# Half-width products and masked copies in the recurrence levels of a hybrid decoder layer

## The chip, the cores and the metric

The kernel runs on one core of one Trainium2 chip. The metric is device time in microseconds (us) of one execution. Before the change three runs gave 2996.32, 3003.64 and 3007.43 us; the median is 3003.64 us. One further execution was profiled and took 3003.55 us, of which 3001.8 us lie between its first and its last instruction (the span).

## The reference, cut to what matters

One decoder layer over 1024 tokens of width 1024: normalise, project to q, f, i, g (four heads of 128 columns each) and u, run a gated linear recurrence (HGRN2) on the heads and a state-space scan (S5) on u, project out, normalise again, and add a mixture of retrieved expert rows (PEER). The change touches only the recurrence of the heads:

```python
f = lb + (1 - lb) * sigmoid(f_logit);  log_f = log(f);  k = 1 - f
bcum = cumsum(lc, axis=2)                    # within a chunk
decay = exp(where(causal, bcum_t - bcum_s, -inf))
scores = einsum('bhtk,bhsk,bhtsk->bhts', qc, kc, decay)
o_intra = einsum('bhts,bhsv->bhtv', scores, vc)
...
new_state = exp(b_last) * state + einsum('bhsk,bhsv->bhkv', kc * exp(b_last - bcum), vc)
o = rmsnorm(o_inter + o_intra) * silu(g)
```

## The kernel before, in words

Tokens are handled in four chunks of 256 columns (`CHUNKS`). `hgrn_in` makes the tiles f, k, b (the running sum of log f), q, gg and v of one piece, `hgrn_out` the recurrence of that piece. A piece is 512 columns wide, which is four blocks (`NB2` = 4) of 128 tokens: one head of chunks 0 and 1 together, or two heads of chunk 2 or 3. So there are eight calls of `hgrn_out`: four for chunks 0 and 1 and two each for chunks 2 and 3.

The scores of a block are a 128 x 128 table (source token s on the partitions, target token t along the columns). Since the decay can't be split into a factor of s and a factor of t without overflow, `hgrn_out` builds the table in eight levels, `a` = 0 to 7. At level a below 7 the tokens are cut into runs of `lsz` = 2^a; pairs of neighbouring runs are treated with the end of the earlier run as reference point. The tile xx holds, in the later run of each pair, q times the decay since the reference point (line 735), and in the earlier run, k times the decay up to it (line 736); at level 0 these are f times q (line 726) and a copy of k (line 727). TensorE multiplies xx with itself, block by block (line 741, tile hg in PSUM), and VectorE copies out of the 128 x 128 result those entries whose s lies in an earlier run and whose t lies in the later run of the same pair, by a mask of bytes, into the table sc (line 742). Level 7 is the diagonal: k times q under the mask of the identity. Two PSUM tiles of the name hg turn over, so the product of level a + 2 waits for the copy of level a. After the levels come the decays over a block (lines 745 to 751), a transpose (754), the state (759 to 767) and the output products (770, 771).

Each float32 product appears in the trace as two matrix instructions, each with its own weight load; 4 blocks x 7 levels x 8 calls = 224 products are 448 instructions, and the diagonal adds 64.

The pieces of chunks 0 and 1 are called between the S5 groups; after that `ORDER` gives the sequence: pieces of chunk 2 beside the output projection and second normalisation of chunk 0 (`o0 N0`), pieces of chunk 3 beside those of chunk 1. That is the order of the calls only: the program is built with `schedule_with_timeline_sim=True`, so a planner with estimated costs sets the order of the instructions on each engine when the kernel is built. Each engine then works its own list in order and waits on semaphores for the others.

Names in the rows below: `proj` (line 326) is every projection with 256 columns; `rstd_fin` (lines 231 to 249) is the chain of small VectorE steps for 1/sqrt; line 272 makes the diagonal matrices `diag` out of it, with which line 286 normalises and transposes; line 807 adds the output projection to x; line 971 is the product of a gathered expert row with h2; lines 1040, 1041 and 1076 belong to the dense part of the experts.

Of the kernel before, what the change touches and what calls it, by code (L numbers as in the profile page):

```python
# [22 lines left out]
P = 128  # L23
# [66 lines left out]
def hymba_kernel(  # L90
# [22 lines left out]
    nc = tc.nc  # L113
# [3 lines left out]
    def T(pool, shape, dt, tag, bufs=None):  # L117
        return pool.tile(shape, dt, name=f"{tag}_{next(cnt)}", tag=tag, bufs=bufs)
# [5 lines left out]
    def bc(ap, axis, n):  # L124
        a = ap.unsqueeze(axis)
        shape = list(a.shape)
        shape[axis] = n
        return a.to_broadcast(shape)
# [81 lines left out]
    def pair(pool, dt=F32, tag="tmp", bufs=4):  # L210
        return T(pool, [P, 2, TC], dt, tag, bufs=bufs)
# [15 lines left out]
    def rstd_fin(pool, ms, n, w):  # L227

        W = lambda dt: T(pool, [P, n], dt, "rstd", bufs=9)
        m = W(F32)  # L230
        TS(m, ms, 1.0 / w, EPS, ALU.mult, ALU.add)
        i = W(I32)
        TS(i, m.bitcast(I32), -0.5, 1597463007.0, ALU.mult, ALU.add)
        y = i.bitcast(F32)
        z = W(F32)
        TT(z, m, y, ALU.mult)
        for r in range(3):
            u = W(F32)
            if r < 2:

                STT(u, z, -0.5, y, ALU.mult, ALU.mult)
            else:
                STT(u, y, -0.5, y, ALU.mult, ALU.mult)
                TT(u, u, m, ALU.mult)
            y2 = W(F32)
            STT(y2, u, 1.5, y, ALU.add, ALU.mult)
            if r == 0:
                z2 = W(F32)
                STT(z2, u, 1.5, z, ALU.add, ALU.mult)
                z = z2  # L250
            y = y2
        return y
# [378 lines left out]
    sts, scs, hc = [], [], {}  # L631
# [34 lines left out]
    NB2 = 2 * NBC  # L666
    B4 = lambda t: t.rearrange("p (c t) -> p c t", t=P)
# [42 lines left out]
    def hgrn_out(hp, last, h, tiles, one, dst):  # L710
        f, k, b, q, gg, v = tiles
        W = lambda tag, bufs=None: T(hp, [P, W2], F32, tag, bufs=bufs or NH.get(tag, 2))
        PB = lambda tag: T(ps, [P, BANK], F32, tag, bufs=2)
        blk = lambda t, c: t[:, c * P : (c + 1) * P]
        sc = scs[0]
        for a in range(8):
            lsz = 1 << a
            pt = PB("hg")
            if a < 7:
                two = lambda t: t.rearrange("p (n two l) -> p n two l", two=2, l=lsz)  # L720
                bv, qv, kv = two(b), two(q), two(k)
                n = W2 // (2 * lsz)
                xx = W("xx")
                xv = two(xx)
                if a == 0:
                    TT(xv[:, :, 1, :], two(f)[:, :, 1, :], qv[:, :, 1, :], ALU.mult)
                    nc.vector.tensor_copy(xv[:, :, 0, :], kv[:, :, 0, :])
                else:
                    z = W("z")
                    zv = two(z)  # L730
                    ref = bv[:, :, 0, lsz - 1 : lsz].to_broadcast([P, n, lsz])
                    TT(zv[:, :, 1, :], bv[:, :, 1, :], ref, ALU.subtract)
                    TT(zv[:, :, 0, :], ref, bv[:, :, 0, :], ALU.subtract)
                    ACT(z, z, AF.Exp)
                    TT(xv[:, :, 1, :], zv[:, :, 1, :], qv[:, :, 1, :], ALU.mult)
                    TT(xv[:, :, 0, :], zv[:, :, 0, :], kv[:, :, 0, :], ALU.mult)
                lh, rh = xx, xx
            else:
                lh, rh = k, q
            for c in range(NB2):  # L740
                nc.tensor.matmul(blk(pt, c), blk(lh, c), blk(rh, c), start=True, stop=True)
            nc.vector.copy_predicated(sc, bc(hc["masks"][:, a, :], 1, NB2), B4(pt))

        e = W("e", 1)
        ACT(e, b, AF.Exp)
        qd = W("xx")
        TT(qd, q, e, ALU.mult)
        z = W("z")
        TT(B4(z), B4(b)[:, :, P - 1 : P].to_broadcast([P, NB2, P]), B4(b), ALU.subtract)
        ACT(z, z, AF.Exp)  # L750
        TT(z, z, k, ALU.mult)
        pk = PB("tr")
        for c in range(NB2):
            nc.tensor.transpose(blk(pk, c), blk(z, c), ident)
        kd = W("kd", 1)
        nc.scalar.copy(kd, pk)
        pst = PB("hg")
        for c in range(NB2):
            nc.tensor.matmul(blk(pst, c), blk(kd, c), blk(v, c), start=True, stop=True)

        sth = W("sth", 1)
        nb = NB2 if one else NBC
        before = []
        for c in range(NB2):
            src = sts[h + c // nb] if c % nb == 0 else blk(sth, c - 1)
            before.append(src)
            STT(blk(sth, c), src, e[:, c * P + P - 1 : c * P + P], blk(pst, c), ALU.mult, ALU.add)
        po = PB("hg")
        for c in range(NB2):
            nc.tensor.matmul(blk(po, c), blk(qd, c), before[c], start=True, stop=False)  # L770
            nc.tensor.matmul(blk(po, c), sc[:, c, :], blk(v, c), start=False, stop=True)
        if not last:
            for i in range(NB2 // nb):
                nc.vector.tensor_copy(sts[h + i], blk(sth, (i + 1) * nb - 1))
        osq = W("z")
        ACT(osq, po, AF.Square)
        ms = T(tp, [P, NB2], F32, "ms", bufs=3)
        nc.vector.tensor_reduce(ms, B4(osq), AX.X, ALU.add)
        r = rstd_fin(tp, ms, NB2, P)
        on = W("xx")  # L780
        TT(B4(on), B4(po), bc(r, 2, P), ALU.mult)
        pt = PB("tr")
        for c in range(NB2):
            nc.tensor.transpose(blk(pt, c), blk(on, c), ident)
        mx = dst if dst is not None else pair(tp, F32, "mixr", 4)
        STT(mx.rearrange("p h t -> p (h t)"), pt, gnw, gg, ALU.mult, ALU.mult)
        return mx
# [49 lines left out]
    for o, i, ni, j, nj in pieces_:  # L837
        n = max(ni, nj)
# [388 lines left out]
    def head_pieces(c, two=False):  # L1227

        t = {}
        outs = []  # L1230
        far = T(gp, [P, 2, 2, TC], F32, "acc") if c == 2 else None

        def last(h):
            outs.append(hgrn_out(hp, c == NCK - 1, h, t.pop(h), two, None if far is None else far[:, h // 2]))
            if not two:
                raws.setdefault(c, []).append((outs[-1][:, 0], outs[-1][:, 1]))

        for h in range(0, HEADS, 1 if two else 2):
            if len(t) == 2:
                last(min(t))  # L1240
                yield
            t[h] = hgrn_in(hp, h, hTs[c], hTs[c + 1] if two else None)
            yield
        for h in sorted(t):
            last(h)
            yield
        if two:
            for i in range(2):
                raws[c + i] = [(outs[h][:, i], outs[h + 1][:, i]) for h in range(0, HEADS, 2)]
# [188 lines left out]
```

## Time and profile before

| | before |
|---|---|
| median of three runs | 3003.64 us |
| profiled execution | 3003.55 us, span 3001.8 us |
| TensorE busy | 2793.9 us, 93% of the span |
| weight loads busy | 2500.6 us, 83% |
| VectorE busy | 2480.9 us, 83% |
| ScalarE busy | 1095.5 us, 36% |
| GpSimd busy | 1108.5 us, 37% |
| mean granted TensorE clock | 0.973 |

How to read it: busy time is the sum over the instructions of an engine, with overlaps counted once. Matrix instructions are pipelined: one takes some 0.275 us from start to end, while the next starts much earlier, so the distance between starts, not the duration, is the price of one. "PE" is TensorE's matrix row, "PEld" its row of weight loads, DVE is VectorE, ACT ScalarE, POOL GpSimd. [...]

### The profile page before, as it was taken

To read this page: it belongs to the slowest core of one execution; us is meant where nothing else is said; L and a number is where in the kernel's file an instruction comes from. 1 tells how busy PE (TensorE), PEld (TensorE's weight loads), DVE (VectorE), ACT (ScalarE), POOL (GpSimd) and SP (SyncE) were. 2 spreads that over 40 slices of the span, in tenths; PEclk is the share of its full clock that TensorE was granted. 3 is DMA by queue.
4 is the path that set the end of the run, shared out by engine and by line. 5 is a ranking of instruction groups with operands and counts; after the bars stand their busy time and mean duration, and the time that the engine had idled before them with its cause. 6 is when DMAs were issued, how large, how long until landed. Compare 5 with 4: busy or idle time off the path is not lost.

```text
span 3001.8 us, 46134 instructions
## 1 busy us (share of the span) xinstructions
PE 2793.9 (93%) x16071; PEld 2500.6 (83%) x16071; DVE 2480.9 (83%) x5606; ACT 1095.5 (36%) x2406; POOL 1108.5 (37%) x1043
## 2 busy tenths in 40 slices
PE   6898979988989799999999999999999999999995
PEld 5677878877878789999998888888888888888874
DVE  7869844987799999997667888888888888888998
ACT  4223431422310688996623322222222222222222
POOL 1764100231112002333344444445545454535553
PEclk9899999999999899999999999999999999999998
DMA  9722334685766358998999999889999898999986
GB/s 335 262 81 66 105 116 155 211 300 189 249 228 187 119 189 305 330 358 320 372 332 352 331 315 329 301 304 360 341 345 317 314 325 310 328 316 329 309 318 231
DMA packets 376265, 816.69 MB, mean 272 GB/s; under 512 B 60128, under 2 KB 153952, under 8 KB 370912
## 3 DMA queue, kind: packets, MB, share of 16 engines
q0 software_dynamic: 110592, 402.70, 38.2%
q1 hardware_dynamic: 227248, 388.74, 37.4%
q10 hardware_dynamic: 38192, 22.31, 2.6%
q8 instruction: 126, 2.06, 0.3%
q14 instruction: 107, 0.88, 0.1%
HBM read 732.27 MB, written 81.36 MB: 271 GB/s over the span
## 4 chain that ended last, share of the span: by engine, by line
PE 35%; DVE 20%; issue 18%; DMA 14%; POOL 10%; ACT 3%; ACTq 0%; POOLq 0%; DVEq 0%; SPq 0%
PE mm L1076 15%; POOL row L946 8%; PE mm L326 8%; DMA row<-in_v_rows_dram,ei 5%; PE s L1152 3%; DVE row L971 3%; PE tr L1152 2%; PE hg L1152 2%; DMA row<-in_u_rows_dram,ei 2%; DMA vraw<-in_v_rows_dram 2%; DVE acc L987 2%; ACT oL L1036 1%; DMA S<-sd 1%; PE s L1040 1%; PE s L1041 1%
## 5 line engine op out<-in xcount | busy, mean ns | idle before, releaser
L1076 PE MATMUL mm<-h2T,w 128*128 128x320 f32 x6144 | 958.7, 315 | 43.2 <-ACT S L1078 33.0
L1076 PEld LDWEIGHTS mm<-h2T,w 128*128 128x128 f32 x6144 | 925.9, 192 | 55.4 <-ACT S L1078 38.8
L946 POOL DMA_INDIRECT row<-in_u_rows_dram,ei x384 | 452.0, 1177 | 1166.8 <-DVE dots L971 711.5
L946 POOL DMA_INDIRECT row<-in_v_rows_dram,ei x384 | 494.8, 1288 | 525.1 <-DVE acc L987 422.5
L326 PE MATMUL mm<-hT,w 128*128 128x256 f32 x2304 | 531.5, 385 | 3.3 <-ACT tmp L610 2.7
L987 DVE SCALAR_TENSOR_TENSOR acc<-row,dots,acc 128x1024 f32<-128x1024 f32 x381 | 487.8, 1280 | 36.4 <-DMA row<-in_v_rows_dram,ei 33.3
L326 PEld LDWEIGHTS mm<-hT,w 128*128 128x128 f32 x2304 | 435.1, 194 | 61.0 <-ACT tmp L610 3.1
L971 DVE CUSTOM_DVE_ANT_0 row<-row,h2n 128x1024 f32<-128x1024 f32 x384 | 462.2, 1216 | 21.3 <-DMA row<-in_u_rows_dram,ei 21.1
L1152 PE MATMUL hg<-v,W 128*128 128x512 f32 x1296 | 351.9, 394 | 16.4 <-DVE v L256 6.9
L255 ACT CAST v<-vraw 128x512 fp32r<-128x512 f32 x256 | 158.4, 620 | 537.5 <-DMA vraw<-in_v_rows_dram 269.3
L1152 PE MATMUL s<-v,W 128*128 128x512 f32 x1296 | 347.7, 391 | 2.9 <-DVE v L256 1.3
L1152 PE MATMUL tr<-v,W 128*128 128x512 f32 x1248 | 336.3, 391 | 4.9 <-DVE v L256 2.9
L1152 PEld LDWEIGHTS hg<-v,W 128*128 128x128 f32 x1296 | 243.4, 189 | 71.8 <-DVE v L256 10.1
L1152 PEld LDWEIGHTS s<-v,W 128*128 128x128 f32 x1296 | 243.2, 188 | 54.9 <-DVE v L256 2.0
L1152 PEld LDWEIGHTS tr<-v,W 128*128 128x128 f32 x1248 | 234.0, 188 | 54.8 <-DVE v L256 4.1
L256 DVE TENSOR_TENSOR w<-raw,w 128x512 fp32r<-128x512 f32 x256 | 175.3, 686 | 96.7 <-ACT w L255 95.3
L256 DVE TENSOR_TENSOR v<-vraw,v 128x512 fp32r<-128x512 f32 x256 | 175.6, 686 | 95.8 <-ACT v L255 95.7
L255 ACT CAST w<-raw 128x512 fp32r<-128x512 f32 x256 | 158.1, 622 | 177.1 <-PE mm L1076 169.5
L1036 ACT ACTIVATE oL<-oA,self 128x128 f16<-128x128 f16 x640 | 196.7, 416 | 4.1 <-DVE self L1022 4.1
L1078 ACT ACTIVATE S<-mm 128x320 f32<-128x320 f32 x256 | 109.5, 439 | 202.9 <-PE mm L1076 169.3
L255 ACT CAST W<-S 128x640 fp32r<-128x640 f32 x128 | 93.3, 730 | 208.8 <-PE s L1152 63.7
L1095 DVE TENSOR_TENSOR S<-S,gt 128x640 f32<-128x640 f32 x128 | 104.3, 819 | 38.4 <-DMA S<-sd 34.7
(373 smaller groups left out, 3151.7 us busy)
## 6 DMA issues: line engine op xcount, KB each, us to landing
raw<-in_u_t_dram SPq DMA_DIRECT2D x256, 256.0 KB, 6.5
vraw<-in_v_rows_dram SPq DMA_DIRECT2D x256, 256.0 KB, 6.5
gd<-Gs SPq DMA_DIRECT2D x40, 1024.0 KB, 7.3
gt<-gd SPq DMA_DIRECT2D x32, 1280.0 KB, 15.6
w<-in_w_in_dram SPq DMA_DIRECT2D x56, 512.0 KB, 4.2
w<-in_w_q_dram SPq DMA_DIRECT2D x48, 512.0 KB, 4.6
sd<-S SPq DMA_DIRECT2D x64, 320.0 KB, 6.0
S<-sd SPq DMA_DIRECT2D x64, 320.0 KB, 8.3
```

The source lines that it names most:

```text
L255: nc.scalar.copy(hi, src)
L256: return nc.vector.tensor_tensor(lo, src, hi.bitcast(F32), ALU.subtract)
L326: ins = nc.tensor.matmul(out, w[:, k * P : (k + 1) * P], rhs[k], start=(k == 0), stop=(k == nk - 1))
L946: g = nc.gpsimd.indirect_dma_start(out=t, out_offset=None, in_=table, in_offset=bass.IndirectOffsetOnAxis(ap=idx, axis=0))
L971: nc.vector.tensor_tensor_reduce(out=ut, in0=ut, in1=h2, scale=1.0, scalar=0.0, op0=ALU.mult, op1=ALU.add, accum_out=dots[:, j : j + 1],)
L987: STT(acc, vt, w[:, j : j + 1], acc, ALU.mult, ALU.add)
L1036: nc.scalar.mul(Al[:, i], at(A, i), sL[:, t8 + i : t8 + i + 1])
L1040: nc.tensor.matmul(pg[:, i - o4, :], at(B, i), at(Ah, i), start=True, stop=False)
L1076: nc.tensor.matmul(pt, wk[:, i, kc], h2T[k][:, j, cs_], start=(n == 0), stop=(n == 3 * KD - 1))
L1078: ACT(g[:, cs_], pt, AF.Gelu)
L1095: TT(gv, gv, gtile[0][:, :, e % IG, :], ALU.mult)
L1152: nc.tensor.matmul(pv[tb], ws[e][:, a, tb * P : (tb + 1) * P], v2[:, b, :], start=(e == s and n == 0), stop=(e == s + SLAB - 1 and n == 2),)
```

## The change

At levels 0 to 6 the product computes only the columns of the later runs, which are the only ones that the copy takes: the moving operand is the later half of xx (64 of the 128 columns of a block, picked with a stride), the result lies packed in 256 columns of the PSUM tile instead of 512, and the masked copy reads these 256, with destination and mask picked by the same stride (`late`). At level 0 the weights are k itself, so the copy of k into xx (line 727) is gone. Level 7 is as before.

```diff
+                late = lambda t: t.rearrange("p c (n two l) -> p c n two l", two=2, l=lsz)[:, :, :, 1, :]
...
                 if a == 0:
                     TT(xv[:, :, 1, :], two(f)[:, :, 1, :], qv[:, :, 1, :], ALU.mult)
-                    nc.vector.tensor_copy(xv[:, :, 0, :], kv[:, :, 0, :])
+                    lh = k
                 else:
+                    lh = xx
...
-                lh, rh = xx, xx
+
+                half = P // 2
+                for c in range(NB2):
+                    nc.tensor.matmul(
+                        pt[:, c * half : (c + 1) * half].rearrange("p (n l) -> p n l", l=lsz), blk(lh, c), two(blk(xx, c))[:, :, 1, :],
+                        start=True, stop=True,
+                    )
+                nc.vector.copy_predicated(
+                    late(sc), late(bc(hc["masks"][:, a, :], 1, NB2)),
+                    pt[:, : NB2 * half].rearrange("p (c n l) -> p c n l", c=NB2, l=lsz),
+                )
             else:
-                lh, rh = k, q
-            for c in range(NB2):
-                nc.tensor.matmul(blk(pt, c), blk(lh, c), blk(rh, c), start=True, stop=True)
-            nc.vector.copy_predicated(sc, bc(hc["masks"][:, a, :], 1, NB2), B4(pt))
+                for c in range(NB2):
+                    nc.tensor.matmul(blk(pt, c), blk(k, c), blk(q, c), start=True, stop=True)
+                nc.vector.copy_predicated(sc, bc(hc["masks"][:, a, :], 1, NB2), B4(pt))
```

Since the planner's costs change with the shapes, it also orders some instructions anew. The lines behind the change move by 11 in the new file: 231 to 272 keep their numbers, 749 is now 760, 751 is 762; the products are on line 742 (levels) and 752 (diagonal), the copies on 746 and 753.

The first place is VectorE's list where the normalisation of chunk 1 (rstd, then diag) runs among the last levels of a piece of chunk 3. Before:

```order
L246 SCALAR_TENSOR_TENSOR rstd_5093<-rstd_5091,rstd_5087 128x2
L249 SCALAR_TENSOR_TENSOR rstd_5095<-rstd_5091,rstd_5089 128x2
L742 COPY_PREDICATED sc_678<-masks_680,hg_5352 128x512
L241 SCALAR_TENSOR_TENSOR rstd_5097<-rstd_5095,rstd_5093 128x2
L246 SCALAR_TENSOR_TENSOR rstd_5099<-rstd_5097,rstd_5093 128x2
L243 SCALAR_TENSOR_TENSOR rstd_5101<-rstd_5099 128x2
L244 TENSOR_TENSOR rstd_5101<-rstd_5101,rstd_5085 128x2
L742 COPY_PREDICATED sc_678<-masks_680,hg_5365 128x512
L246 SCALAR_TENSOR_TENSOR rstd_5104<-rstd_5101,rstd_5099 128x2
L272 TENSOR_SCALAR diag_5106<-ident_69,rstd_5104 128x128
L272 TENSOR_SCALAR diag_5108<-ident_69,rstd_5104 128x128
```

And with the change:

```order
L241 SCALAR_TENSOR_TENSOR rstd_5091<-rstd_5089,rstd_5087 128x2
L246 SCALAR_TENSOR_TENSOR rstd_5093<-rstd_5091,rstd_5087 128x2
L746 COPY_PREDICATED sc_678<-masks_680,hg_5332 128x8x32
L758 TENSOR_TENSOR xx_5366<-q_4773,e_5364 128x512
L762 TENSOR_TENSOR z_5368<-z_5368,k_4746 128x512
L243 SCALAR_TENSOR_TENSOR rstd_5095<-rstd_5093 128x2
L746 COPY_PREDICATED sc_678<-masks_680,hg_5345 128x4x64
L244 TENSOR_TENSOR rstd_5095<-rstd_5095,rstd_5079 128x2
L246 SCALAR_TENSOR_TENSOR rstd_5098<-rstd_5095,rstd_5093 128x2
L272 TENSOR_SCALAR diag_5100<-ident_69,rstd_5098 128x128
L272 TENSOR_SCALAR diag_5102<-ident_69,rstd_5098 128x128
L753 COPY_PREDICATED sc_678<-masks_680,hg_5358 128x512
```

The masked copy of the diagonal (the second hg before, the last one now) stood ahead of the last rstd step and now stands behind the two diag; the copies left of the chain are the narrow form (256 elements); and the steps of 512 columns on the old lines 747 and 751, which stood a few rows ahead of the piece shown before, now stand within it.

The second place is TensorE's list in the first piece (chunks 0 and 1, a head beside the S5 tables and scans), as a difference; mm is a projection, tr a transpose.

```order
-L741 MATMUL hg_1764<-xx_1765 128x128
+L742 MATMUL hg_1764<-xx_1765,k_1264 128x64
 L705 MATMUL tr_1598<-ident_69,sf_1596 128x128
 L533 MATMUL tr_1486<-ca_1445,bb_1412 16x128
 L705 MATMUL tr_1598<-ident_69,sf_1596 128x128 x3
-L741 MATMUL hg_1764<-xx_1765 128x128 x2
-L741 MATMUL hg_1773<-xx_1774 128x128 x4
-L326 MATMUL mm_2085<-hT_548,w_563_2086 128x256 x2
+L742 MATMUL hg_1764<-xx_1765,k_1264 128x64 x2
+L742 MATMUL hg_1772<-xx_1773 128x64 x4
```

Each product of 128 columns is replaced by one of 64 at the same place; at level 0 its weights are k instead of xx.

## Rows read from the trace of the kernel before

**Rows 1.** The head of the page and its first part (busy time, share of the span and instructions of each engine), and from its second part the busy tenths of TensorE and VectorE in 40 slices of 75 us.

```profile
span 3001.8 us, 46134 instructions
...
PE 2793.9 (93%) x16071; PEld 2500.6 (83%) x16071; DVE 2480.9 (83%) x5606; ACT 1095.5 (36%) x2406; POOL 1108.5 (37%) x1043
...
PE   6898979988989799999999999999999999999995
...
DVE  7869844987799999997667888888888888888998
```

**Rows 2.** Busy time of each engine in five stretches (from and to in us, length, then each engine's busy us with its instructions, the granted TensorE clock as a share of full speed, the DMA share and GB/s).

```profile
195.00:350.00 155.00, 139.64 (x872) 119.65 (x871) 138.60 (x303) 61.76 (x91) 68.30 (x99) 1.00 0.25 73
400.00:450.00 50.00, 41.77 (x229) 37.57 (x230) 22.72 (x73) 12.52 (x29) 0.00 (x0) 0.91 0.34 116
600.00:675.00 75.00, 66.91 (x346) 58.31 (x345) 60.38 (x137) 21.39 (x31) 27.93 (x27) 0.95 0.87 300
675.00:700.00 25.00, 17.88 (x102) 16.00 (x101) 19.48 (x54) 8.68 (x16) 3.56 (x3) 0.80 0.34 118
1000.00:1200.00 200.00, 178.63 (x1441) 171.85 (x1438) 189.67 (x681) 166.28 (x490) 17.43 (x16) 0.94 0.58 209
```

**Rows 3.** The chain of waits that ended last, its shares by engine and line, for the four stretches 195 to 350, 350 to 450, 600 to 700 and 725 to 800 us, in this order; "sc L742" is the masked copy, "hg L741" the products of the levels.

```profile
by line: issue 12.7%; DMA bcin<-in_s5bc_dram 6.0%; PE mm L326 5.6%; DVE z L733 5.1%; DVE sc L742 5.0%; PE hg L741 5.0%; DVE xx L736 3.0%; DVE z L732 2.8%; DVE xhs L573 2.8%; DVE xr L562 2.3%; DVE uc L492 2.2%; PE tr L286 2.2%; POOL us L491 
by line: PE mm L326 36.7%; PE hg L741 10.9%; DMA yt<-ys 9.8%; issue 4.0%; DVE sc L742 4.0%; ACTq L600 2.9%; DMA ys<-h2n 2.2%; PE tr L1189 2.0%; ACT yt L603 1.9%; ACT L603 1.7%; DVE xx L736 1.6%; PE tr L286 1.5%; PE tr L804 1.3%; ACT L734 1.
by line: issue 25.8%; PE mm L326 17.9%; POOL row L946 14.4%; DMA row<-in_u_rows_dram,ei 14.1%; DVE sc L742 4.6%; PE tr L286 3.6%; DVE row L971 3.6%; PE hg L741 3.0%; DVE xh L807 2.6%; DVE xx L736 1.4%; DVE b L698 1.2%; DVE z L733 1.1%; DVE 
by line: PE mm L326 51.7%; DMA w<-in_w_out_dram 6.3%; DVE row L971 4.5%; issue 3.8%; DVE sc L742 2.6%; PE s L863 2.4%; DVE xx L736 2.3%; PE hg L771 2.1%; PE hg L770 2.1%; PE tr L804 2.0%; DVE xx L735 1.9%; DVE mixr L786 1.9%; ACT L734 1.8%;
```

**Rows 4.** Groups of instructions by line, engine, operation and form: count, busy us, mean ns of one, idle time before them and what ended it.

```profile
L741 PE MATMUL hg<-xx 128*128 128x128 f32 x448 | 63.4, 287 | 14.7 <-DVE xx L736 9.2 <-DVE rstd L233 5.1
L742 DVE COPY_PREDICATED sc<-masks,hg 128x512 f32<-128x512 uint8 x64 | 46.3, 723 | 9.5 <-PE hg L741 9.5
L726 DVE TENSOR_TENSOR xx<-f,q 128x256 f32<-128x256 f32 x8 | 3.3, 415 | 0.0
L747 DVE TENSOR_TENSOR xx<-q,e 128x512 f32<-128x512 f32 x8 | 5.4, 676 | 0.0
L727 DVE COPY xx<-k 128x256 f32<-128x256 f32 x8 | 2.4, 299 | 0.0
L1076 PE MATMUL mm<-h2T,w 128*128 128x320 f32 x6144 | 958.7, 315 | 43.2 <-ACT S L1078 33.0
```

**Rows 5.** Groups of weight loads (PEld), the same columns: 16 columns in float32, 128 columns in float32, 128 columns in float16.

```profile
L533 PEld LDWEIGHTS tr<-ca,bb 128*16 128x16 f32 x48 | 3.2, 95 | 7.1 <-issue 3.2 <-DVE mixr L786 2.0 <-DVE ca L493 0.3
L741 PEld LDWEIGHTS hg<-xx 128*128 128x128 f32 x448 | 59.3, 201 | 18.8 <-issue 11.4 <-DVE xx L736 5.1 <-PE hg L741 0.6
L1041 PEld LDWEIGHTS <-oB 128*128 128x128 f16 x640 | 63.3, 99 | 6.6 <-issue 6.1
```

**Rows 6.** Instructions in order of time (start us, duration us, engine, line, operation, tiles, count): the eight product instructions of one level in a row; then a run of float16 products (line 1041, 128 columns) that is followed by float32 ones (line 1076, 320 columns), with one, and with two of the latter in the row; then the weight loads of these, one and two in the row.

```profile
636.60 1.05 PE L741 MATMUL hg<-xx 128*128 128x128 f32 x8
...
1092.77 0.22 PE L1040 MATMUL s<-oH,oB 128*128 128x128 f16 x1
1092.83 0.22 PE L1041 MATMUL s<-oL,oB 128*128 128x128 f16 x1
1092.85 0.39 PE L1076 MATMUL mm<-h2T,w 128*128 128x320 f32 x1
...
1092.85 0.54 PE L1076 MATMUL mm<-h2T,w 128*128 128x320 f32 x2
...
1092.83 0.19 PEld L1076 LDWEIGHTS mm<-h2T,w 128*128 128x128 f32 x1
...
1092.83 0.30 PEld L1076 LDWEIGHTS mm<-h2T,w 128*128 128x128 f32 x2
```

**Rows 7.** Instructions in order of time in the two stretches in which the normalisation of chunk 0 (434 to 449 us) and of chunk 1 (674 to 693 us) runs among levels of a piece; in square brackets the idle time of the engine before the row and what ended it.

```profile
434.97 0.73 DVE L742 COPY_PREDICATED sc<-masks,hg 128x512 f32<-128x512 uint8 x1 [3.16 <-PE hg L741]
...
440.75 0.15 DVE L231 TENSOR_SCALAR rstd<-ms 128x2 f32<-128x2 f32 x1
...
446.13 0.72 DVE L742 COPY_PREDICATED sc<-masks,hg 128x512 f32<-128x512 uint8 x1 [0.32 <-PE hg L741]
...
447.51 0.48 DVE L272 TENSOR_SCALAR diag<-ident,rstd 128x128 f32<-128x128 f32 x2
...
447.86 0.71 PE L286 MATMUL tr<-diag,xh 128*128 128x128 f32 x4 [1.77 <-DVE diag L272]
...
674.66 0.73 DVE L742 COPY_PREDICATED sc<-masks,hg 128x512 f32<-128x512 uint8 x1 [0.37 <-PE hg L741]
...
683.78 0.17 DVE L231 TENSOR_SCALAR rstd<-ms 128x2 f32<-128x2 f32 x1
...
687.44 0.73 DVE L742 COPY_PREDICATED sc<-masks,hg 128x512 f32<-128x512 uint8 x1 [0.82 <-PE hg L741]
...
690.73 0.72 DVE L742 COPY_PREDICATED sc<-masks,hg 128x512 f32<-128x512 uint8 x1
...
691.52 0.48 DVE L272 TENSOR_SCALAR diag<-ident,rstd 128x128 f32<-128x128 f32 x2
...
691.86 1.05 PE L286 MATMUL tr<-diag,xh 128*128 128x128 f32 x4 [2.01 <-DVE diag L272]
```

## The prediction

> **What bounds the kernel now.** I read the head of the page first, then the busy time by stretches, the chain of waits in the stretches where the levels run, the groups of the lines that change, and last single instructions in order of time. TensorE is busy for 2793.9 us of a span of 3001.8 us, VectorE for 2480.9 us [rows 1]. The forty slices show that TensorE is at nine tenths from the fifteenth slice (1050 us) on, and that its gaps lie nearly all ahead of that [rows 1]. The levels run from 195 to 775 us, so the change works among the gaps. From 195 to 350 us both engines are near their limit, TensorE 139.64 and VectorE 138.60 of 155 us; from 400 to 450 us TensorE has 41.77 of 50 us, from 675 to 700 us 17.88 of 25 us, at a granted clock of 0.91 and 0.80 [rows 2]. What takes TensorE's time in these two is seen in order of time: the chain from rstd to diag of chunk 0 begins at 440.75 us and ends at 447.51 us, that of chunk 1 runs from 683.78 to 691.52 us, and the normalisation products wait behind them for 1.77 and 2.01 us [rows 7]. The small steps of that chain stand in VectorE's list between masked copies and other steps of the levels; whatever VectorE drops there, TensorE gets back at once. The chain of waits says the same: the masked copy holds 5.0% of 155 us, 4.0% of 100 us, 4.6% of 100 us and 2.6% of 75 us, together 7.8 + 4.0 + 4.6 + 2.0 = 18.4 us of the copies' 46.3 us [rows 3, 4]. So 40% of their time is on the path that sets the end.
>
> **The copies.** 56 of the 64 copies take 256 elements in place of 512 (the diagonal's eight stay). No row shows such a copy. A two-operand step takes 676 ns at 512 elements and 415 ns at 256, and the latter takes every second element [rows 4]: 261 ns for 256 elements, with no surcharge for the stride. I take 723 - 261 = 462 ns. The ends: no gain (723 ns), if the skipped columns cost as much as the used ones; 299 ns, the cheapest 256-element step of the rows (line 727). The sum off VectorE is 56 x 0.261 = 14.6 us, with ends of 0 and 56 x 0.424 = 23.7 us. A price above 723 ns I leave out, as half the elements are read and the strided step shows no penalty. On the path stand 18.4 of 46.3 us, and the copies as a group get shorter by 14.6 / 46.3 = 32%: 18.4 x 0.32 = 5.8 us.
>
> **The copy of k.** Eight steps of 299 ns are gone, 2.4 us [rows 4]. They stand in the same list; at the same 40% they give 1.0 us.
>
> **What moves.** In the chain of chunk 1 the diagonal's copy now comes behind the diag steps (the first place shown), and the list has the same at chunk 0. Each takes one copy of 0.72 us from in front of the waiting products [rows 7], so 2 x 0.72 = 1.4 us. It isn't free for the piece: the product of the scores with v needs that copy, and it now waits for 0.48 us of diag more, but behind it stands the other half of a piece while TensorE has the normalisation to do. Nothing is added to any queue of transfers; the planner also drops one table load on ScalarE, which has time to spare there (61.76 of 155 us busy [rows 2]), and I count it at nothing. In the later stretch from 1000 to 1200 us, where VectorE is busy for 189.67 and TensorE for 178.63 of 200 us [rows 2], the order of expert products against one-hot products changes as well. The same instructions stand there in another order; I count it at nothing, with 5 us either way, a quarter of TensorE's 21 idle us there.
>
> **The products.** 448 instructions go from 128 columns to 64. Eight of a level take 1.05 us, the last of them some 0.28, so they start 0.11 us apart [rows 4, 6]. By columns that would halve to 0.055 and give 448 x 0.055 = 24.6 us. But each instruction has its own weight load of 128 float32 columns, and this is not half as long. One load in a row lasts 0.19 us and two last 0.30, so loads start 0.11 us apart even where the product before takes less [rows 6]: the float16 products there follow each other by 0.06 us (1092.77, 1092.83), and the first float32 product behind them shows 0.39 us, against a mean of 0.315 for its line [rows 4, 6]. It stood 0.07 us for its weights. And a load of 16 columns takes 95 ns where one of 128 takes 201 [rows 5], so the load goes by its columns. The weights keep their 128 columns, so the pace stays at about 0.11 us: a load can hide behind the product in front of it, not shorten. Ends: 24.6 us if the load were hidden after all; at the other end nothing, since a strided read even at half speed would still end within 0.11 us. I take the near end, 1 us (0.002 us each, within the rounding of the rows), and 0.4 us of it on the path.
>
> [...]
>
> **The sum.** 5.8 + 1.0 + 1.4 + 0.4 = 8.6 us. What is late next: from 195 to 350 us a transfer (bcin, 6.0% of the chain [rows 3]), which the change doesn't touch; the copies' share there is 7.8 x 0.32 = 2.5 us, of which I take only a little as lost, and 8.5 us in all. The profiled execution took 3003.55 us, 0.1 us below the median of the runs: 3003.5 - 8.5 = 2995 us. Within this case the ends are 1 us (copies without gain leave 1.0 + 1.4 + 0.4 = 2.8 us, and the order takes some 2 back) and 17 us (copies at 299 ns give 18.4 x 23.7 / 46.3 = 9.4 us, with the 2.8 and 5 us from the order), so 2986 to 3002 us.
>
> **Rivals.** First, the products do get faster, the weight load hiding behind them: the products hold 5.0% of 155, 10.9% of 100 and 3.0% of 100 us on the chain [rows 3], 21.7 us, half of which would be 10.8 us more: 2995 - 10.8 = 2984 us. For it speaks the share of the chain; against it the 0.39 us in rows 6. Chance 0.11. Second, VectorE's time doesn't reach the end: the places fill with waits for bcin, for the expert rows (14.1% of the chain from 600 to 700 us is their transfers, 25.8% is issue [rows 3]) and for ScalarE, and the order of the later stretch takes back the rest: 3002 us. Against it stand the two waits for diag, which have VectorE alone before them. Chance 0.19. Third, slower: the product instructions keep their pace, but half of it is now waiting for weights, and the granted clock falls from 195 to 350 us, where it is now 1.00 [rows 2]. If it went to 0.91, as from 400 to 450 us, 18% of 155 us would be at the half level, 28 us, with 14 us of product time lost and 0.9 of it felt where TensorE is 90% busy: 12.6 us; with the gain of 8.5 us that is 3008 us. It decides from 19 us more at the half level on (8.5 / 0.45). For it speaks that the clock is lowest where TensorE pauses; against it that the levels' products are only 5.0% of that stretch's chain, and 256-column projections stand between them. Chance 0.10.
>
> **How the numbers follow.** 0.60 for the forecast, 0.11, 0.19 and 0.10 for the rivals. About 0.5% (15 us) is what a measurement of this kernel can tell from no change, the three runs before lying 11 us apart. The forecast's own range crosses 2988.6 us with about a sixth of its chance (0.10); the first rival lies beyond it with nearly all of its own, 0.10: faster 0.21. Beyond 3018.7 us lies a third of the third rival, and a shuffle of the later order worse than I price it: slower 0.05. The rest, 0.74, is no change. The range runs from 2980 (the first rival and the forecast's lower end) to 3008 us (the third).
>
> **What would show it.** The narrow copies near 462 ns, at every level alike; the product instructions of the levels 0.11 us apart as before, with their weight loads at about 190 ns; the diag of chunks 0 and 1 some 2 us nearer to the first copy ahead of them; the clock from 195 to 350 us still 1.00. Copies above 600 ns, or products 0.06 us apart, would make the working wrong; a VectorE sum lower by 17 us with a time unchanged would speak for the second rival.

## The result, and the profile after

The changed kernel takes 2981.99 us (median of 5 runs, 2974.75 to 2988.83) against 3003.64 us: a ratio of 0.992, 95% interval 0.9904 to 0.9936, 21.7 us less. It stayed in the range and went the way that was forecast, but the gain is two and a half times the 8.5 us. The profiled execution of the changed kernel is the fastest of its five, 2974.75 us, so the two profiles lie 28.8 us apart. The head and the busy times, answering to [rows 1]:

```profile
span 2973.0 us, 46130 instructions
...
PE 2782.4 (94%) x16071; PEld 2492.3 (84%) x16071; DVE 2464.2 (83%) x5598; ACT 1093.4 (37%) x2405; POOL 1143.7 (38%) x1043
```

VectorE dropped by 16.7 us, close to the 17 us expected; TensorE by 11.5 us, which none of the forecast's terms would give. The groups, answering to [rows 4] and [rows 5] (the levels now stand on line 742, the narrow copy on 746, the diagonal's on 753, the up-products on 1087):

```profile
L746 DVE COPY_PREDICATED sc<-masks,hg 128x256 f32<-128x256 uint8 x56 | 28.7, 513 | 12.3 <-PE hg L742 12.3
L753 DVE COPY_PREDICATED sc<-masks,hg 128x512 f32<-128x512 uint8 x8 | 5.8, 729 | 3.0 <-PE hg L752 2.9
...
L742 PE MATMUL hg<-xx 128*128 128x64 f32 x384 | 53.9, 290 | 12.2 <-DVE xx L738 10.7 <-DVE rstd L236 1.5
L742 PEld LDWEIGHTS hg<-xx 128*128 128x128 f32 x384 | 53.0, 210 | 15.3 <-issue 9.0 <-DVE xx L738 3.9 <-PE hg L742 1.0
...
L1087 PE MATMUL mm<-h2T,w 128*128 128x320 f32 x6144 | 943.5, 312 | 37.0 <-ACT S L1089 26.2 <-DVE h2T L256 6.6 <-ACT h2T L255 1.9
```

The products kept their pace (111 to 112 ns from start to start in both kernels, median over all pairs of a level) and their weight loads last 210 ns where they lasted 201. The last row shows where time went that no term spoke of: the up-products, which nothing in the change touches, take 15.2 us less than in [rows 4] and TensorE idles 6.2 us less in front of them. In order of time (start and duration), of the first piece of chunk 2 the copies at runs of 2 and of 4 columns, then the chain of chunk 0 that [rows 7] show from before:

```profile
428.56 0.74 DVE L746 COPY_PREDICATED sc<-masks,hg 128x256 f32<-128x256 uint8 x1 [3.11 <-PE hg L742]
...
429.79 0.43 DVE L746 COPY_PREDICATED sc<-masks,hg 128x256 f32<-128x256 uint8 x1
...
434.73 0.16 DVE L231 TENSOR_SCALAR rstd<-ms 128x2 f32<-128x2 f32 x1
...
439.17 0.48 DVE L272 TENSOR_SCALAR diag<-ident,rstd 128x128 f32<-128x128 f32 x2
...
439.51 1.22 PE L286 MATMUL tr<-diag,xh 128*128 128x128 f32 x4
439.68 0.73 DVE L753 COPY_PREDICATED sc<-masks,hg 128x512 f32<-128x512 uint8 x1
```

From rstd to diag it is now 4.4 us instead of 6.8 (chunk 1: 677.67 to 683.45, 5.8 instead of 7.7), and TensorE doesn't wait for diag any more. The masked copy has two prices: over all pieces the median is 723 and 718 ns at runs of 1 and 2 columns, as for 512 elements, and 424 to 440 ns from runs of 4 on. The same stretches as [rows 2]:

```profile
195.00:350.00 155.00, 144.75 (x906) 125.99 (x905) 133.87 (x307) 66.23 (x97) 70.39 (x99) 0.99 0.27 81
...
400.00:450.00 50.00, 47.10 (x262) 42.00 (x261) 15.14 (x49) 14.64 (x32) 0.00 (x0) 0.93 0.36 127
...
600.00:675.00 75.00, 66.35 (x347) 58.84 (x347) 58.12 (x132) 22.59 (x32) 25.52 (x24) 0.91 0.78 267
675.00:700.00 25.00, 22.01 (x109) 19.23 (x108) 12.83 (x39) 10.13 (x20) 3.56 (x3) 0.73 0.45 149
...
1000.00:1200.00 200.00, 185.69 (x1533) 179.59 (x1532) 191.52 (x672) 173.30 (x522) 23.17 (x20) 0.97 0.63 227
```

From 1000 to 1200 us TensorE does 92 instructions more, at a clock of 0.97 instead of 0.94. Matching the same TensorE instructions of both profiles, the changed kernel is ahead by 8.5 us (median of the instructions in a stretch) from 950 to 1000 us, as forecast, but by 14 us at 1200, 18 at 1550, 22 at 1750 and 29 to 35 us from 2000 us on. Two thirds of the gap in these profiles opened where nothing but the order differs.

### The profile page after: what moved, and what is told of

It reads as the page before. It is cut to its first block, busy times and chain, and to the rows that moved or that the text cites. A ratio compares the mean times of both kernels' runs of the same rounds, so it can differ in the third digit from the quotient of the medians.

```text
span 2973.0 us, 46130 instructions
## 1 busy us (share of the span) xinstructions
PE 2782.4 (94%) x16071; PEld 2492.3 (84%) x16071; DVE 2464.2 (83%) x5598; ACT 1093.4 (37%) x2405; POOL 1143.7 (38%) x1043
## 4 chain that ended last, share of the span: by engine, by line
PE 33%; DVE 19%; issue 19%; DMA 15%; POOL 10%; ACT 4%; POOLq 0%; ACTq 0%; DVEq 0%; SPq 0%
PE mm L1087 10%; PE mm L326 10%; POOL row L957 8%; DMA row<-in_v_rows_dram,ei 7%; PE hg L1163 3%; PE s L1163 3%; PE tr L1163 2%; DVE row L982 2%; DVE acc L998 2%; DMA row<-in_u_rows_dram,ei 2%; ACT oL L1047 2%; DMA vraw<-in_v_rows_dram 2%; DMA S<-sd 1%; DVE v L256 1%; PE hg L742 1%
## 5 line engine op out<-in xcount | busy, mean ns | idle before, releaser
L1087 PE MATMUL mm<-h2T,w 128*128 128x320 f32 x6144 | 943.5, 312 | 37.0 <-ACT S L1089 26.2
L1087 PEld LDWEIGHTS mm<-h2T,w 128*128 128x128 f32 x6144 | 913.9, 189 | 47.6 <-ACT S L1089 31.3
L957 POOL DMA_INDIRECT row<-in_v_rows_dram,ei x384 | 523.2, 1363 | 486.5 <-DVE acc L998 400.4
L998 DVE SCALAR_TENSOR_TENSOR acc<-row,dots,acc 128x1024 f32<-128x1024 f32 x381 | 487.7, 1280 | 44.6 <-DMA row<-in_v_rows_dram,ei 41.3
```

Of the source, the lines that this page charges most:

```text
L957: g = nc.gpsimd.indirect_dma_start(out=t, out_offset=None, in_=table, in_offset=bass.IndirectOffsetOnAxis(ap=idx, axis=0))
L998: STT(acc, vt, w[:, j : j + 1], acc, ALU.mult, ALU.add)
L1087: nc.tensor.matmul(pt, wk[:, i, kc], h2T[k][:, j, cs_], start=(n == 0), stop=(n == 3 * KD - 1))
```

## The experiments

Two things changed together: the instructions of the levels, and the order that the planner then chose for every engine. They were taken apart by holding a kernel to a list. Behind the trace of the program, each engine's instructions get issue-order edges along a recorded list (of the kernel before, or of the changed one); no wait on a semaphore is added:

```diff
+    pin_order(tc, nc, gone)   # last line of hymba_kernel
...
+            if last is not None:
+                tc.add_manual_dep(
+                    i, last.name, mybir.DependencyInfo(mybir.DependencyClass.NoSync, mybir.DependencyReason.DATA), reason="issue order",
+                )
+            last = i
```

My first theory: the shorter copies reach the end, in the old order too. The rival: the gain is the planner's. A control, the kernel before held to its own list, was not run; that the edges cost no time by themselves is read from run 2, which has such edges and is as fast as the changed kernel, which has none. (Such a kernel's lines carry higher numbers, because the lists stand in its file.) Each timing is of 6 to 12 executions beside 19 to 29 of the kernel before, whose median was 3005 to 3009 us.

**1. The new instructions in the old order** (the changed kernel, held to the list of the kernel before).

> The instructions of the changed kernel, but every engine is held to the order that the kernel before has (by issue-order edges alone; the eight copies of k are left out of it). Theory O (about 8 us come from the shorter copies up to 800 us, and the rest from the planner's new order behind that): 2992 to 2997 us against 3003.6 before. Theory S (the order is worth nothing; what starts 8 us earlier collects the rest by itself): 2980 to 2985 us, as the changed kernel.

Measured: 3005.1 us, ratio 1.0004 (0.9988 to 1.0019). No gain, where both theories had one.

**2. The old instructions in the new order** (the kernel before, held to the list of the changed one).

> The instructions of the kernel before, full-width products and copies, held to the order of the changed kernel (the copies of k stand behind the step they followed). Theory O: 2988 to 2993 us, that is 10 to 15 us faster than before though no instruction is shorter. Theory S: 3000 to 3006 us, no change.

Measured: 2981.2 us, ratio 0.9931 (0.9906 to 0.9955). The whole gain comes with not one instruction made shorter, more than theory O had given the order. Its row of up-products:

```profile
L1259 PE MATMUL mm<-h2T,w 128*128 128x320 f32 x6144 | 944.9, 313 | 36.0 <-ACT S L1261 25.7 <-DVE h2T L439 6.2 <-ACT h2T L438 1.7
```

In run 1, which has the old order, the same row is:

```profile
L1272 PE MATMUL mm<-h2T,w 128*128 128x320 f32 x6144 | 955.8, 314 | 38.8 <-ACT S L1274 28.5 <-DVE h2T L441 6.3 <-ACT h2T L440 1.8
```

**3. As run 1, but the products of levels 1 to 6 wide again**, so that, but for level 0, only the copies are narrow:

```diff
+                wide = a > 0
                 for c in range(NB2):
+                    if wide:
+                        nc.tensor.matmul(blk(pt, c), blk(lh, c), blk(xx, c), start=True, stop=True)
+                        continue
...
-                    pt[:, : NB2 * half].rearrange("p (c n l) -> p c n l", c=NB2, l=lsz),
+                    late(B4(pt)) if wide else pt[:, : NB2 * half].rearrange("p (c n l) -> p c n l", c=NB2, l=lsz),
```

> As new_code_old_order, but the products of levels 1 to 6 take all 128 columns again and the copy picks its 256 elements from PSUM with a stride. If the weight load sets the pace of a product (0.11 us at 64 and at 128 columns): within 2 us of new_code_old_order, and the products 0.11 us apart in both. If narrow products are cheaper on the path: 5 to 12 us slower than new_code_old_order. A strided read of PSUM that is slower would show in the copies' duration.

Measured: 2997.9 us, ratio 0.998 (0.9963 to 0.9997), and a second time:

> The changed kernel in the old order with wide products, once more: 2995 to 3002 us, a ratio of 0.997 to 0.999 and a mean clock of 0.973 or more, if the narrow copies are worth some 6 us there; 3003 to 3008 if the first result was chance.

3001.3 us, 0.9979 (0.9961 to 0.9997). Neither expectation named this. In the old order the narrow copies and the missing copies of k are worth 6 us, and the narrow products take them back: the twelve executions of run 3 are 7.3 us shorter in the mean than the twelve of run 1 beside them, give or take 4.4 us (two standard errors). The products are no slower, the step stays at 112 ns in all four kernels, and the copies take 510 ns on average with the strided read of PSUM and 511 without. What differs is the granted clock. The mean over the timed executions was 0.968 in run 1, 0.974 and 0.973 with wide products, 0.973 in the kernel before. The stretches 400 to 450 and 675 to 700 us of run 1:

```profile
400.00:450.00 50.00, 43.33 (x225) 39.08 (x225) 20.21 (x64) 11.64 (x27) 0.00 (x0) 0.84 0.33 116
...
675.00:700.00 25.00, 18.66 (x112) 16.97 (x112) 23.16 (x65) 9.20 (x15) 3.64 (x4) 0.78 0.38 141
```

The same of run 3:

```profile
400.00:450.00 50.00, 43.42 (x235) 38.83 (x236) 19.56 (x61) 12.21 (x28) 0.00 (x0) 0.91 0.33 116
...
675.00:700.00 25.00, 18.39 (x131) 15.96 (x129) 20.50 (x60) 11.13 (x20) 4.49 (x4) 1.00 0.46 159
```

Summed from 195 to 725 us, the time lost below full speed (one minus the clock, times the length) is 22 to 32 us in the six profiles with narrow products, mean 26.2, and 14 to 22 us in the twelve with wide ones, mean 19.5. The loss of some 7 us in the old order is clear of the noise, and so is the lower clock; that the one comes by way of the other is likely, but was not shown apart.

**4. The price of the masked copy.** As run 1, with the mask bytes of the late columns packed into a table of their own (by seven small steps of VectorE more):

```diff
-                    late(sc), late(bc(hc["masks"][:, a, :], 1, NB2)),
+                    late(sc), bc(hc["packed"][:, a, :], 1, NB2).rearrange("p c (n l) -> p c n l", l=lsz),
```

> As new_code_old_order, but the byte masks of the later runs lie packed (64 bytes a level), so the copy reads them without a stride; the table is still written with the stride. In the changed kernel the copies of levels 0 and 1 take 0.72 us and those of levels 2 to 6 0.43 us. If the mask's short runs of bytes cause that: 0.43 us at all levels, 16 x 0.29 = 4.6 us less on VectorE and 1 to 3 us less in all. If the strided write of the table causes it: 0.72 us stay at levels 0 and 1 and the time is that of new_code_old_order.

Measured: 3008.8 us, ratio 1.0009 (0.999 to 1.0028); 718 and 714 ns at runs of 1 and 2, 419 to 437 ns from 4 on. So it isn't the mask alone. Then, at these two levels, the table and the mask in one piece of 64 columns a block (the entries of these levels then stand in the wrong places):

```diff
+                if a < 2:
+                    nc.vector.copy_predicated(
+                        sc[:, :, :half], bc(hc["masks"][:, a, :half], 1, NB2),
+                        pt[:, : NB2 * half].rearrange("p (c t) -> p c t", c=NB2),
+                    )
+                    continue
```

> The changed kernel in the old order, but the masked copies at runs of 1 and 2 write the first 64 columns of each chunk of the table in one piece, by one piece of mask, in place of every other run (this leaves the table's entries of these two levels wrong; the work is the same in size). Their duration, 0.72 us with the mask bytes spaced and with them packed, 0.43 us at longer runs: if the spaced table write costs it, these copies fall to about 0.43 us; if it is the place of these levels in the program or the size, they stay at 0.72. The time is expected at 2997 to 3012, as of the changed kernel in the old order, by both.

One execution, 3005.95 us. The copies of levels 0 and 1 now have a row of their own, line 932, beside those of the other levels, line 937:

```profile
L937 DVE COPY_PREDICATED sc<-masks,hg 128x256 f32<-128x256 uint8 x40 | 17.2, 430 | 4.5 <-PE hg L927 4.5
L932 DVE COPY_PREDICATED sc<-masks,hg 128x256 f32<-128x256 uint8 x16 | 6.9, 430 | 3.1 <-PE hg L927 3.1
```

So the copies fall from 0.72 us to 430 ns. As a packed mask alone changed nothing and PSUM is packed in both, what is left is the table written in runs of 1 or 2 float32, or the fine pattern of the instruction as a whole; these two weren't separated.

**5. Which stretch of the new order?** The kernel before, held to the new list in one stretch and to its own elsewhere; the cuts lie where the same instructions stand ahead of them in both.

> The instructions of the kernel before; every engine takes the order of the changed kernel up to TensorE's matmul 2026 (806 us of the profile before) and the old order behind it. The whole new order gave -20 us with these instructions. Theory 'late': the gain comes from the order behind 806 us, so here at most -4 us, 2999 to 3006. Theory 'early': the heads' new order starts all that follows sooner, and the rest follows in step: 2985 or less.

Measured: 3000.3 us, ratio 0.9979 (0.9964 to 0.9993).

> The instructions of the kernel before; new order only for what stands between TensorE's matmuls 2026 and 4561 (806 to 1274 us), where the first up-products come some 30 places earlier among the gate map's products. Theory 'late, in the mixed stretch': -6 to -12 us, about 2994 to 3000, and a DMA share in 1000 to 1200 us that rises from 0.58. Theory 'early', or 'behind 1274 us': within 4 us of the kernel before.

Measured: 2998.4 us, 0.9972 (0.9955 to 0.999).

> The instructions of the kernel before; new order only from TensorE's matmul 4561 on (1274 us). Theory 'late, behind 1274 us' (the loads of the up-products' and v weights are issued in another order, SyncE's rows there differ): -8 to -14 us, 2990 to 2998. Theory 'early' or 'mixed stretch': within 4 us of the kernel before. If the parts add up, the three runs' differences sum to -20 us; if none has it alone, the gain needs the stretches together.

Measured: 2997.9 us, 0.9961 (0.9939 to 0.9983). By the ratios that is 6, 8 and 12 us, 26 us together (by the medians 5, 7 and 8, together 20) against the 21 to 27 us of the whole order: the parts add up within their intervals, and neither 'early' nor 'late' has it alone. The DMA share from 1000 to 1200 us, expected to rise in the middle run, stayed (0.59). In the middle stretch ScalarE's step on the gate map (Gs) came sooner. TensorE's waits from 1000 to 1280 us, first of the kernel before, then of the kernel with the new order in this stretch (us in all, times, longest):

```profile
PE s L1040 <- ACT Gs L1043: 4.6, 3, 3.0
```

```profile
PE s L1225 <- ACT Gs L1228: 1.2, 1, 1.2
```

The last stretch was cut once more, because it holds one large move (the gate map's products go some 14 places back behind up-products) and many of one to three places:

> The instructions of the kernel before; new order only between TensorE's matmuls 4561 and 7134 (1274 to 1627 us), where the gate map's products move some 14 places back behind up-products. Theory 'one move, of the gate map behind the experts': most of the late gain, -6 to -10 us, 2995 to 2999. Rival 'many small moves': -2 to -5 us, 3000 to 3004.

Measured: 3003.4 us, ratio 0.9984 (0.9969 to 0.9999).

> The instructions of the kernel before; new order only from TensorE's matmul 7134 on (1627 us), where steps move by one to three places. Theory 'one move, of the gate map': within 2 us of the kernel before, 3003 to 3008. Rival 'many small moves': -4 to -7 us, 2998 to 3002, with TensorE's waits from 1550 to 2050 us below the 18.8 us of before.

Measured: 3002.8 us, 0.998 (0.9966 to 0.9995). Again both, 5 and 6 us, each with an interval that ends just below 1; the single large move doesn't have it alone, 'many small moves' stands, though its run was expected at 3002 at most. TensorE's waits behind 1627 us show what such moves do. From 1550 to 2050 us, of the kernel before:

```profile
PE mm L1076 <- ACT S L1078: 10.4, 5, 3.9
PE hg L1152 <- ACT v L255: 4.5, 1, 4.5
```

and of the changed kernel:

```profile
PE mm L1087 <- ACT S L1089: 5.7, 5, 1.6
PE tr L1163 <- DVE dacc L1176: 4.0, 1, 4.0
PE hg L1163 <- ACT v L255: 1.6, 1, 1.6
```

The moves save waits and make others (4.0 us for VectorE's dacc, 0.3 us before): all of TensorE's waits there come to 18.8 us before, 12.4 in the changed kernel and 13.4 in the last run. Which engine's list carries it wasn't tried.

**6. The new order with wide products, and all versions side by side.** The changed kernel with the edit of run 3, in its own order:

> The changed kernel in its own order, with the products of levels 1 to 6 at 128 columns as before; the masked copies stay at 256 elements and read every other run from PSUM. In the old order this edit took the mean granted clock from 0.968 to 0.974 and 7 us off. Theory 'the narrow products lower the clock': the same here, mean clock 0.976 or more against 0.974, and 5 to 8 us under the changed kernel, 2974 to 2978. Rival 'the clock difference belonged to the old order': as the changed kernel, 2980 to 2984, clock 0.974.

> The changed kernel as it is, for comparison on the same chip: 2978 to 2986 us, mean clock 0.974, by every theory.

Measured: 2978.4 us (0.9907, 0.9882 to 0.9932), mean clock 0.977, against 2978.0 us (0.9901, 0.9883 to 0.992), mean clock 0.9735, of the changed kernel. The clock rises as in the old order, the time doesn't move: my theory of the clock falls for this order. Once more, in a later session:

> The changed kernel with the products of levels 1 to 6 at 128 columns, once more beside it: mean clock 0.977 against 0.974. If TensorE's lost clock sets the end in this order too: 3 to 8 us under the changed kernel. If it doesn't, as the first time: within 2 us of it.

> The changed kernel as it is: 2976 to 2984 us, mean clock 0.973 to 0.975.

> The instructions of the kernel before in the order of the changed kernel, once more, now on one chip with the changed kernel. If the shorter copies and the missing copies of k are worth in the new order what they were worth in the old one (6 us, with wide products): 4 to 8 us over the changed kernel. If the new order has taken over what they gave: within 2 us of it.

Measured: 2982.5 us (0.9928, 0.9904 to 0.9952) and mean clock 0.976 with wide products, 2982.5 (0.9911, 0.9882 to 0.9941) and 0.974 for the changed kernel, 2982.1 (0.9911, 0.9886 to 0.9936) for the old instructions. In the new order no form of the instructions tells from another, but these are 6 to 8 executions each: the two pairs with wide products together lie 2 us above the changed kernel, give or take 5, and the old instructions 1 us above it, give or take 6.5 (two standard errors). No version beat the changed kernel.

## Why the prediction was wrong

**The order.** The step that failed stands under "What moves": the order of the later stretch was counted "at nothing, with 5 us either way". It measured 8 us from 806 to 1274 us and, behind that, where no term stood at all, another 11 to 12 us. I priced a shuffle by the instructions it moves, and they are the same. What it changes is how often TensorE pauses and what it pays afterwards. The up-products tell it. One lasts 309 ns (median), but some last 468 ns, in twelve runs of 7 to 20 before and six of 7 to 14 after, each at most ten TensorE instructions behind a pause of over 0.5 us. All of them, 148 before and 60 after, lie where the granted clock is at half of full speed (in both profiles it is at 1.00 or at 0.50 throughout); no up-product wholly at that half level takes less than 400 ns. One such place in the kernel before: an up-product waits 3.94 us for ScalarE, and half a microsecond after TensorE has begun again the clock falls to 0.50. The windows show the stretch with the pause, the one at the half level and the one behind it (TensorE's busy time and instructions come first, the clock third from the end):

```profile
1879.43 6.80 PE L1076 MATMUL mm<-h2T,w 128*128 128x320 f32 x34 [3.94 <-ACT S L1078]
```

```profile
1876.00:1879.90 3.90, 0.47 (x3) 0.47 (x4) 1.65 (x3) 1.47 (x4) 0.00 (x0) 1.00 0.46 180
1880.00:1883.30 3.30, 3.30 (x14) 3.30 (x14) 3.30 (x5) 1.36 (x3) 1.14 (x1) 0.50 0.47 127
1883.40:1890.00 6.60, 6.60 (x47) 6.60 (x46) 6.15 (x8) 2.00 (x4) 3.45 (x3) 1.00 0.78 227
```

From start to start an up-product takes 267 ns at the half level and 147 ns at full speed. The 88 slow ones fewer are thus worth 10.6 us; with 6.2 us less idle time in the same row that is 17 of the 28.8 us between the two profiles. It isn't a matter of these two alone: from 990 to 2870 us the seven profiles with the old order behind 806 us are at the half level for 41 to 68 us (mean 60.5), the seven with the whole new order for 27 to 44 (mean 33.2), and the four with the new order in one later stretch for 44 to 55. As the traces read, such a pause of TensorE costs its own length (3.94 us in the place shown) and then the slow products behind it (12 there, each 120 ns more), and moves of a few places that bring ScalarE's results sooner can save both. That the pauses bring the clock down was not tried by itself.

**The copies.** 462 ns at every level alike was wrong in form: 424 to 440 at five levels, 0.72 us at two, 513 on average. Off VectorE went 40.5 - 28.7 = 11.8 us instead of 14.6; that its sum fell by 16.7 us, as expected, is chance, since 2.5 us of that lie in other steps. The share of the path agrees: 40% of 11.8 us and 1.0 us for the copies of k give 5.7 us, and the old order with wide products measured 6. In the new order no such gain was seen (the old instructions end with the new ones), but 6 us could hide in the noise of that comparison.

**The diagonal's copy.** Right: both diag came some 2 us nearer and both waits are gone. It is part of the 6 us that the new order gives ahead of 806 us, where 1.4 us were forecast.

**The products.** The pace stayed, as worked out, and the first rival is out: 111 to 112 ns from start to start (median) at 64 and at 128 columns, and the weight loads of the levels, 128 columns in both kernels, start 112 ns apart in both. That the loads set the pace agrees with this, but was not shown apart. The "near end, 1 us" missed their price: with half the columns at the same pace the mean clock in the old order was 0.968, with the wide products 0.974 and 0.973. That is the fall of the clock that the third rival named; that it comes from waiting for weights was not shown. Its place was only half right: from 195 to 350 us the six profiles with narrow products lost 1.7 to 5.1 us of full speed, mean 4.3, the twelve with wide ones 0 to 3.4, mean 2.0, so most of the loss lies behind that. Its threshold, 19 us more at the half level, is just reached: over 195 to 725 us the three profiles with narrow products in the old order lost 29.0 us of full speed on average, the seven with wide ones in that order there 19.3, so 9.7 us, or 19 us at the half level, and there the gain was indeed eaten up. In the new order the same difference is 3.5 us of full speed. The second rival's outcome, about no gain (3002 us), is what the instructions alone came to (ratio 1.0004), by a cause that it didn't name.

**The sum.** 8.5 us were to come from the instructions and nothing from the order. Measured: about nothing from the instructions (6 from the copies, as much back with the narrow products, in the old order), 21 us and more from the order. The 8.5 us by which the changed kernel leads at 1000 us agree with the forecast in number only. That the time lies within 2980 to 3008 us is luck: the range reached down to 2980 by the first rival, whose faster products are not there. The chance of 0.21 for faster was too small because both ends of the order's term were taken from one stretch.

## What to carry to other kernels

Where a planner sets the order, a change of a few durations re-deals every engine's list down to the end, and the re-deal may be worth more than the change: compare the lists over the whole program, price a reordered stretch by its idle time and its slow products together (6.2 and 10.6 us here), and keep the range wide enough for it. That the re-deal came out faster here is chance as far as these runs show. To learn what the edit itself is worth, hold the new instructions to the old order and the old ones to the new. Making the products narrower without making them faster (112 ns apart at 64 columns as at 128) was no saving here.

## What the runs showed that was not expected

A masked copy of 256 elements into every other run of a float32 table takes 0.72 us at runs of 1 and 2 elements, as much as 512 elements in one piece, and 0.43 us at runs of 4 and more; packing the mask doesn't help, writing the table in pieces of 64 with a mask in such pieces does (0.43 us). A two-operand step at runs of 1 showed no such charge (415 ns for 256 elements, 676 for 512 in one piece) [rows 4]. And products of 64 columns that start 112 ns apart like those of 128 lower TensorE's mean granted clock, by 0.005 in the old order and 0.002 to 0.004 in the new one, where it cost no time that these runs could show. An up-product of 320 columns starts 147 ns behind the one before it at the full granted clock (1.00) and 267 ns at the half level (0.50).
